# Modulation columns in 512-wide units and a new product order in the token-major groups of a hybrid decoder kernel

## The chip, the core and the metric

The kernel runs on one core of a Trainium2 chip. Time is device time of one launch in microseconds (us); the figure quoted for a kernel is the median of its runs. The core has five engines with instruction queues of their own: TensorE (PE in the rows, its weight loads as PEld), VectorE (DVE), ScalarE (ACT), GpSimd (POOL) and SyncE (SP, which here issues nearly all transfers).

## The reference, cut to what matters

One decoder layer on a sequence of 1024 tokens with 1024 features, all in 32-bit floats:

```python
mod = silu(c) @ w_ada + b_ada                    # 6 x 1024 columns of modulation
sh_a, sc_a, gt_a, sh_f, sc_f, gt_f = split(mod, 6)
h = rms_norm(x) * (1 + sc_a) + sh_a
proj = h @ w_in                                  # 9224 columns, split into:
aq, ak, av, mq, mk, mv, mo, mi, mf, ga, gm       # attention, mLSTM, gates
ya = differential_attention(aq, ak, av)
ym = sigmoid(mo) * mlstm(silu(conv(mq, mk)), mv, mi, mf)
x = x + gt_a * ((sigmoid(ga) * (ya @ w_a) + sigmoid(gm) * (ym @ w_m)) @ w_out)
h = rms_norm(x) * (1 + sc_f) + sh_f
x = x + gt_f * (relu(h @ w_ff1)**2 @ w_ff2)
```

The change touches two things: the product `h @ w_in` for the columns `mv`, `mo` and `av`, and the last 4096 of the 6144 columns of `mod` (`gt_a`, `sh_f`, `sc_f`, `gt_f`), which are needed only after the mixers.

## The kernel before

**Stages.** Up to 75.56 us the kernel normalizes x, transposes it, makes the first 2048 modulation columns (`sh_a`, `sc_a`) and, beside these, one column group of `mo` directly (`first_unit`, with its bank `ops`). From 75.56 to 306.92 five *token-major groups* (class `Tok`) compute the other columns of `mv`, `mo` and `av`. Then come eleven groups of class `Conv` and `Gate` (columns `mq`, `mk`, `ga`, `gm`, with the convolution's taps on VectorE beside them) to about 520, four mLSTM heads to about 800, eight attention heads to about 1250, the merge, and the MLP from 1430 to the end.

**A group.** Each of the groups multiplies a 1024 x 512 or 1024 x 256 block of `w_in` with h by seven half-size products in place of eight (a Strassen-type scheme, class `Group`). Products 1, 2 and 3 use quarters of the data as they are, 4 to 7 sums and differences of them, on both sides. Every operand is split into a high and a low half in TensorE's reduced 32-bit format: ScalarE copies the value into the high half (line 320), VectorE subtracts that from the value (line 138, called from `parts`). The three matmuls high x high, high x low, low x high (line 328, in `mm_block`) then give nearly full precision. In a `Tok` group a product is two halves n = 0, 1 of 24 matmuls each, 48 matmuls of 128 x 256.

**Left operands.** The weight quarters a11, a12, a21, a22 are loaded into four tiles `w_st` (line 395; two of them from a pool of two, two from the pool "b"). `weights` makes the operands in the order in which the products run: 5, 6, 3 and 7 need an addition or subtraction first (lines 411 to 419). Operands `w_op` lie in a ring of four, so operand k+4 can be made when product k has ended. The difference for product 7 goes into `cr[0]` (method `s3` of `Tok`).

**Right operands.** `B[1]` to `B[3]` are views of h transposed. Those of 7, 5, 6 and 4 are made once by `right` (lines 1393 to 1412: subtractions at line 313 on tiles `xT`, then `parts` into tiles `t7`, `t5`, `t6`, `t4`), ahead of the first group and in the same queues.

**Results.** Product 1 leaves its bank `pa` by a ScalarE copy into `m1` (line 431), and product 2 adds onto the bank. Product 7 leaves `pc` by a copy into `m7` (line 443); product 5 leaves its bank by a VectorE addition into `m7` (line 449); product 6 is added to `m1` (line 455) and yields the first output. Product 3 then accumulates on the bank `pb` of product 5, and product 4 on `pc` of product 7. The first group runs 1, 2, 7, 5, 6, 3, 4, the four others 1, 7, 2, 5, 6, 3, 4.

**Further modulation columns.** `ada_unit` (lines 695 to 740) makes 256 columns: two loads of 512 KB, each into the one buffer `cr[1]` (line 711), eight VectorE steps that multiply and add the rows into `ac` (lines 715 and 717, 256 wide), and, in `total`, a matmul with ones that sums over the partitions (line 725 or 731). There are 16 units. Fourteen are placed in the `Tok` groups, one gather for every second product; the last two stand in the first two mLSTM heads.

**What sets the order.** Every engine runs its queue in order. The order in the queues is fixed when the kernel is built: a scheduler places the instructions by program order and readiness, and pools hand out a buffer when its last reader is done. `weave` strings the steps of two lists together, here one product with one entry of `extra`.

## Time and profile before

| | |
|---|---|
| runs | 2082.44, 2076.57, 2079.22 us (median 2079.22) |
| profiled execution | 2075.06 us, its span 2073.0 us |
| mean granted clock of TensorE | 0.979 |
| TensorE busy | 1989.1 us |
| VectorE busy | 1655.4 us |
| ScalarE busy | 1045.0 us |

The span is the time from the first to the last instruction in the trace of the one execution that was profiled; that execution's own time is 2.06 us more. Times in the rows count from the start of the span. The profile gives busy time by engine and stretch, timelines of single engines, and for idle time what ended it. The granted clock is the share of TensorE's full speed that the chip's throttle allowed in a stretch.

### The profile page before, as it was taken

The numbers are of one execution on the slowest core, as the hardware profiler recorded it, in microseconds if no ns is written. First come the engines' busy times: TensorE is split into PE (matmuls) and PEld (weight loads), VectorE is DVE, ScalarE is ACT, GpSimd is POOL, SyncE is SP. The second block draws the span as 40 slices with busy tenths as digits, with TensorE's granted clock in tenths as the row PEclk, the third lists the DMA queues.
The fourth block names the chain that finished last, engine by engine and source line by source line (L and its number), as shares of the span: only waits on it lengthen the run. The fifth ranks groups of instructions, "written<-read, shape, count | busy, mean of one in ns | idle before, by whom it ended". The sixth has DMA issues, their size and how long they took to land.

```text
span 2073.0 us, 30238 instructions
## 1 busy us (share of the span) xinstructions
PE 1989.1 (96%) x11201; PEld 1723.2 (83%) x11201; DVE 1655.4 (80%) x2964; ACT 1045.0 (50%) x1966; POOL 59.3 (3%) x154
## 2 busy tenths in 40 slices
PE   5899999999999999999999899999899999999999
PEld 5899998888787899999999788777678887788887
DVE  7976768889676568999978657999867667998896
ACT  5522324544566557877767634456445445433332
POOL 0000000000011000000000110000000000000000
PEclk7999999999999999999999999999999999999999
DMA  8354452333765442322222665513444446744532
GB/s 283 107 173 157 146 180 101 102 112 134 219 207 169 138 126 54 85 77 82 62 64 85 198 226 168 185 41 112 162 153 153 146 148 235 275 154 159 163 107 77
DMA packets 210633, 296.71 MB, mean 143 GB/s; under 512 B 14067, under 2 KB 132494, under 8 KB 210486
## 3 DMA queue, kind: packets, MB, share of 16 engines
q1 hardware_dynamic: 207542, 285.35, 43.2%
q0 software_dynamic: 2944, 9.44, 1.2%
q8 instruction: 88, 1.44, 0.3%
q14 instruction: 59, 0.48, 0.1%
HBM read 206.43 MB, written 79.93 MB: 138 GB/s over the span
## 4 chain that ended last, share of the span: by engine, by line
PE 62%; DVE 15%; DMA 11%; issue 6%; ACT 4%; POOL 1%; SPq 0%; DVEq 0%; POOLq 0%; ACTq 0%
PE cps L328 15%; PE pb L328 8%; PE pc L328 7%; PE pa L328 7%; PE pd L328 4%; DMA crow<-in_w_ada_dram 4%; PE ps L166 3%; PE ps L165 3%; PE ps L167 3%; PE lg L1190 3%; PE pv L1243 3%; DVE ac L717 2%; DMA ex<-ea_d 1%; PE tp L1223 1%; PE ops L579 1%
## 5 line engine op out<-in xcount | busy, mean ns | idle before, releaser
L328 PE MATMUL cps<-t_op,s_op 128*128 128x512 f32 x2016 | 471.9, 395 | 10.6 <-ACT s_op L320 5.2
L328 PEld LDWEIGHTS cps<-t_op,s_op 128*128 128x128 f32 x2016 | 379.1, 189 | 100.8 <-ACT s_op L320 6.5
L320 ACT ACTIVATE w_op<-w_st 128x512 fp32r<-128x512 f32 (+1 forms) x192 | 130.6, 695 | 179.8 <-PE pb L328 62.6
L138 DVE TENSOR_TENSOR w_op<-w_st,w_op 128x512 fp32r<-128x512 f32 (+1 forms) x192 | 144.3, 770 | 8.3 <-ACT w_op L320 6.4
L165 PE MATMUL ps<-w_hi,hT 128*128 128x256 f32 x512 | 146.5, 286 | 0.0
L166 PE MATMUL ps<-w_lo,hT 128*128 128x256 f32 x512 | 145.9, 285 | 0.0
L167 PE MATMUL ps<-w_hi,hT 128*128 128x256 f32 x512 | 145.7, 284 | 0.0
L320 ACT ACTIVATE s_op<-act 128x1024 fp32r<-128x1024 f32 x56 | 58.6, 1052 | 143.4 <-PE cps L328 107.6
L328 PE MATMUL pc<-bt,w_op 128*128 128x512 f32 x384 | 99.8, 407 | 6.1 <-ACT w_op L320 5.1
L1200 ACT ACTIVATE ee<-ee,mneg 128x256 f32<-128x256 f32 (+7 forms) x128 | 98.2, 769 | 9.8 <-DVE mneg L1196 9.5
L1190 PE MATMUL lg<-kb,qe 128*128 128x512 f32 (+3 forms) x384 | 96.7, 360 | 3.2 <-DVE mneg L1196 2.5
L166 PEld LDWEIGHTS ps<-w_lo,hT 128*128 128x128 f32 x512 | 97.6, 191 | 1.3 <-issue 0.9
L165 PEld LDWEIGHTS ps<-w_hi,hT 128*128 128x128 f32 x512 | 97.6, 191 | 0.5
L167 PEld LDWEIGHTS ps<-w_hi,hT 128*128 128x128 f32 x512 | 97.6, 191 | 0.3
L328 PEld LDWEIGHTS pc<-bt,w_op 128*128 128x128 f32 x384 | 73.7, 195 | 27.2 <-ACT w_op L320 6.0
L328 PE MATMUL pa<-b,w_op 128*128 128x512 f32 x384 | 94.3, 396 | 0.7 <-DVE w_op L138 0.7
L316 DVE TENSOR_TENSOR acc<-cps,acc 128x512 f32<-128x512 f32 x116 | 76.9, 684 | 13.6 <-PE cps L328 13.5
L328 PEld LDWEIGHTS pa<-b,w_op 128*128 128x128 f32 x384 | 72.7, 190 | 16.1 <-DVE w_op L138 1.0
L717 DVE SCALAR_TENSOR_TENSOR ac<-crow,cond,ac 128x256 f32<-128x256 f32 x112 | 54.0, 482 | 29.5 <-DMA crow<-in_w_ada_dram 27.8
L1196 DVE CUSTOM_DVE_ANT_0 ee<-lg,bs 128x512 f32<-128x512 f32 (+4 forms) x128 | 69.9, 559 | 8.8 <-PE lg L1190 7.8
L138 DVE TENSOR_TENSOR s_op<-act,s_op 128x1024 fp32r<-128x1024 f32 x56 | 68.2, 1219 | 5.9 <-ACT s_op L320 5.9
L1190 PEld LDWEIGHTS lg<-kb,qe 128*128 128x128 f32 x384 | 61.5, 192 | 11.0 <-DVE mneg L1196 6.3
(406 smaller groups left out, 4798.8 us busy)
## 6 DMA issues: line engine op xcount, KB each, us to landing
w_st<-in_w_in_dram SPq DMA_DIRECT2D x72, 512.0 KB, 4.4
act<-act_d SPq DMA_DIRECT2D x56, 512.0 KB, 4.4
w_st<-in_w_ff_dram SPq DMA_DIRECT2D x36, 512.0 KB, 4.1
crow<-in_w_ada_dram SPq DMA_DIRECT2D x32, 512.0 KB, 4.2
w<-in_w_ff_dram SPq DMA_DIRECT2D x32, 512.0 KB, 4.9
act_d<-s SPq DMA_DIRECT2D x48, 256.0 KB, 2.0
wa<-in_w_ada_dram SPq DMA_DIRECT2D x16, 512.0 KB, 4.8
mq_d<-cv SPq DMA_DIRECT2D x16, 512.0 KB, 2.6
```

The source lines that it names most:

```text
L138: return (nc.gpsimd if pool else nc.vector).tensor_tensor(dst, src, hi.bitcast(F32), op=ALU.subtract)
L165: nc.tensor.matmul(o, lhsT=ah, rhs=bh, start=first, stop=False)
L166: nc.tensor.matmul(o, lhsT=ah, rhs=bl, start=False, stop=False)
L167: nc.tensor.matmul(o, lhsT=al, rhs=bh, start=False, stop=last)
L316: (nc.gpsimd if pick(pool, n) else nc.vector).tensor_tensor(o, a, b, op=ALU.add)
L320: nc.scalar.activation(dst[0], src, AF.Copy)
L328: nc.tensor.matmul(ps, lhsT=p, rhs=q, start=first and k == 0 and r == 0, stop=k == 3 and r == 2, skip_group_check=True,)
L717: nc.vector.scalar_tensor_tensor(ac, stv[:, k, :], cond[:, kk:kk + 1], ac, op0=ALU.mult, op1=ALU.add)
L1190: nc.tensor.matmul(lg[:, 0:max(256, w)], lhsT=hd["q"][hf][e][:, r, q4 * P:(q4 + 1) * P], rhs=hd["k"][e][:, c0:c0 + max(256, w)], start=r = ...
L1196: nc.vector.tensor_tensor_reduce(ee[:, c0:c0 + w], lg[:, 0:w], hd["bs"][:, n - c0 - w:n - c0][:, ::-1], -0.125, first, ALU.add, ALU.min, last,
L1200: nc.scalar.activation(ee[:, 0:n], ee[:, 0:n], AF.Exp, bias=mneg[:, e:e + 1], scale=-1.0, accum_out=ssum[:, e:e + 1])
L1243: nc.tensor.matmul(pv[:, 0:256], lhsT=pts[kk // 4][r][:, (kk % 4) * P:(kk % 4 + 1) * P], rhs=v, start=kk == 0 and r == 0, stop=kk == qi an ...
```

## The change

1. The further columns are made in 8 units of 512 columns. A unit has four loads of 512 KB (256 rows x 512 columns), alternately into `cr[0]` and `cr[1]`, and four `gather` steps of two VectorE instructions each, 512 wide. One load, one gather and, for every fourth, one total are placed at each product: `fetch(q)` two products ahead of `gather(q)`. Three of these steps fall into the first `Conv` group, and none is left in the mLSTM heads.
2. All `Tok` groups run the products in the order 1, 2, 5, 6, 3, 7, 4. ScalarE copies product 5 out of its bank into `m7`; VectorE adds product 7 to that from `pc`; the output that needs both is written behind product 7.
3. The difference for product 7 is made in a11's own tile (a22 - a11, where a11 holds a21 - a11 by then), so `cr[0]` is no longer used for it.
4. The first group's loads and operands are called earlier, between the calls of `right`.
5. `gate_rows` writes two tiles of 512 instead of one of 1024.

```diff
+        late7 = False
...
-                if i == 7:
+                if i == 7 and self.late7:
+                    src = a11
+                    sub(a11, a22, a11, *p, n=n)
+                elif i == 7:
...
-        gs = wt("b", [16, S], "gs")
         for i in range(2):
-            nc.scalar.copy(gs[:, i * 512:(i + 1) * 512], gps[i][0:16, :])
-        nc.sync.dma_start(gs_d, gs)
+            gs = wt("f", [16, 512], "gs")
+            nc.scalar.copy(gs, gps[i][0:16, :])
+            nc.sync.dma_start(gs_d[:, i * 512:(i + 1) * 512], gs)
...
+        def fetch(q):
+            stv = cr[q % 2].rearrange("p (k c) -> p k c", k=2)
+            src = w_ada[0][q * 256:(q + 1) * 256, c0:c0 + 512].rearrange("(k p) c -> p k c", p=P)
+            nc.sync.dma_start(stv, src)
+
+        def gather(q):
+            stv = cr[q % 2].rearrange("p (k c) -> p k c", k=2)
+            if not q:
+                box.append(wt("f", [P, 512], "ac"))
+            ac = box[0]
+            for k in range(2):
+                f = cond[:, q * 2 + k:q * 2 + k + 1]
+                if q or k:
+                    nc.vector.scalar_tensor_tensor(ac, stv[:, k, :], f, ac, op0=ALU.mult, op1=ALU.add)
+                else:
+                    nc.vector.tensor_scalar(ac, stv[:, k, :], f, None, op0=ALU.mult)
...
-        def s3(self):
-            return cr[0].rearrange("p (k c) -> p k c", k=4)
+        late7 = True
+        def p5(self):
+            for n in self.ns:
+                self.pb[n] = bank("pa", "pb5")
+                self.m7[n] = wt("m", [P, 512], "m7")
+                self.prod(5, n, self.pb[n], True)
+                nc.scalar.activation(self.m7[n], self.pb[n], AF.Copy)
+        def p6(self):
+            for n in self.ns:
+                pd, m1 = bank("mm", "pd"), self.m1[n]
+                self.prod(6, n, pd, True)
+                add(m1, pd, m1, False)
+        def p7(self):
+            for n in self.ns:
+                m7 = self.m7[n]
+                self.pc[n] = bank("pb", "pc")
+                self.prod(7, n, self.pc[n], True)
+                add(m7, self.pc[n], m7, False)
+                self.out(1, 1, n, m7, self.m1[n], m7)
...
+    ORDER_T = (1, 2, 5, 6, 3, 7, 4)
+    first_tok = Tok(*toks[0])
     right(7, "vvvv")
+    first_tok.load()
     right(5, "eeee")
+    first_tok.weights(ORDER_T[0:2])
     half(1)
     gate_rows(gps)
     right(6, "rrrr")
+    first_tok.weights(ORDER_T[2:6])
     right(4, "rruu")
+    first_tok.weights(ORDER_T[6:])
...
-    extra = [[] for _ in range(7 * len(toks))]
-    na = 0
-    while na < 16 and na * 2 + 7 < len(extra):
-        extra[na * 2].append(ada[na][0])
-        extra[na * 2 + 7].append(ada[na][1])
-        na += 1
+    extra = [[] for _ in range(7 * len(toks) + 3)]
+    for u, (fetch, gather, total) in enumerate(ada):
+        for q in range(4):
+            extra[2 + u * 4 + q].append(lambda f=fetch, q=q: f(q))
+            extra[4 + u * 4 + q].insert(0, lambda f=gather, q=q: f(q))
+        extra[8 + u * 4].insert(0, total)
...
-        more = ada[na + h::MH]
-        for u, (gather, total) in enumerate(more):
-            filler.insert(len(filler) * (2 * u + 1) // (2 * len(more) + 1), gather)
-            filler.insert(len(filler) * (2 * u + 2) // (2 * len(more) + 1), total)
```

VectorE, first group: the low half of the second product's weights (`w_op_774` before, `w_op_612` after) among the output-gate steps `mo` and the steps for right operands (`xT`, `t6`, `t4`). Before:

```order
L604 TENSOR_SCALAR mo_653<-mo_653 128x512
L604 TENSOR_SCALAR mo_689<-mo_689 128x512
L604 TENSOR_SCALAR mo_717<-mo_717 128x512
L313 TENSOR_TENSOR xT12_121<-xT12_121,xT02_119 128x1024
L313 TENSOR_TENSOR xT13_122<-xT13_122,xT03_120 128x1024
L138 TENSOR_TENSOR t6_737<-xT12_121,t6_735 128x2x256
L313 TENSOR_TENSOR xT10_123<-xT10_123,xT12_121 128x1024
L138 TENSOR_TENSOR t6_738<-xT12_121,t6_736 128x2x256
L138 TENSOR_TENSOR t6_737<-xT13_122,t6_735 128x2x256
L138 TENSOR_TENSOR t6_738<-xT13_122,t6_736 128x2x256
L313 TENSOR_TENSOR xT11_124<-xT11_124,xT13_122 128x1024
L138 TENSOR_TENSOR w_op_774<-w_st_767,w_op_774 128x1024
```

The same place after:

```order
L138 TENSOR_TENSOR w_op_612<-w_st_591,w_op_612 128x1024
L610 TENSOR_SCALAR mo_667<-mo_667 128x512
L610 TENSOR_SCALAR mo_703<-mo_703 128x512
L610 TENSOR_SCALAR mo_731<-mo_731 128x512
L313 TENSOR_TENSOR xT12_121<-xT12_121,xT02_119 128x1024
L313 TENSOR_TENSOR xT13_122<-xT13_122,xT03_120 128x1024
L138 TENSOR_TENSOR t6_753<-xT12_121,t6_751 128x2x256
L316 TENSOR_TENSOR w_st_588<-w_st_588,w_st_592 128x1024
L138 TENSOR_TENSOR t6_754<-xT12_121,t6_752 128x2x256
L138 TENSOR_TENSOR t6_753<-xT13_122,t6_751 128x2x256
L138 TENSOR_TENSOR t6_754<-xT13_122,t6_752 128x2x256
L138 TENSOR_TENSOR w_op_763<-w_st_588,w_op_763 128x1024
```

The second product's low half moved from behind eleven of these steps to ahead of them, and product 5's addition (`w_st_588`) and low half (`w_op_763`) now stand among the right operands.

VectorE, second group: reads of product 5 (`m7<-pb5`, before) and of product 7 (`m7<-pc`, after) out of their banks, between steps of the modulation columns (`ac<-crow`) and operands (`w_op`, `w_st`). Before:

```order
L717 SCALAR_TENSOR_TENSOR ac_1208<-crow_762,cond_96,ac_1208 128x256 x3
L726 TENSOR_TENSOR ac_970<-adp_1430,ac_970 128x256
L138 TENSOR_TENSOR w_op_1250<-w_st_1225,w_op_1250 128x1024
L717 SCALAR_TENSOR_TENSOR ac_1208<-crow_762,cond_96,ac_1208 128x256 x3
L316 TENSOR_TENSOR m7_1312<-pb5_1434,m7_1312 128x512
L717 SCALAR_TENSOR_TENSOR ac_1208<-crow_762,cond_96,ac_1208 128x256
L316 TENSOR_TENSOR w_st_1679<-w_st_1679,w_st_1683 128x1024
L316 TENSOR_TENSOR m7_1339<-pb5_1460,m7_1339 128x512
```

After, in the same group from product 3's second addition (`c<-pb5`) on:

```order
L316 TENSOR_TENSOR c_1503<-pb5_1367,m1_1247 128x512
L722 TENSOR_SCALAR ac_1567<-crow_796,cond_96 128x512
L138 TENSOR_TENSOR w_op_1641<-w_st_1634,w_op_1641 128x1024
L720 SCALAR_TENSOR_TENSOR ac_1567<-crow_796,cond_96,ac_1567 128x512
L313 TENSOR_TENSOR w_st_1634<-w_st_1634,w_st_1630 128x1024
L316 TENSOR_TENSOR m7_1341<-pc_1511,m7_1341 128x512
L720 SCALAR_TENSOR_TENSOR ac_1567<-crow_797,cond_96,ac_1567 128x512
L316 TENSOR_TENSOR m7_1341<-m7_1341,m1_1220 128x512
L316 TENSOR_TENSOR m7_1368<-pc_1539,m7_1368 128x512
```

VectorE no longer reads product 5 at all; it reads product 7, with single modulation steps ahead of the two reads, and those steps now come from two buffers (`crow_796`, `crow_797`).

## Rows read from the trace of the kernel before

**Rows 1.** The page's part 1: engine, busy us (share of span), instructions.

```profile
PE 1989.1 (96%) x11201; PEld 1723.2 (83%) x11201; DVE 1655.4 (80%) x2964; ACT 1045.0 (50%) x1966; POOL 59.3 (3%) x154
```

**Rows 2.** Stretches: us, busy us (instructions) by engine, granted clock, DMA share, GB/s.

```profile
95.00:310.00 215.00, 205.43 (x1643) 203.36 (x1642) 149.38 (x249) 55.52 (x74) 3.43 (x6) 0.97 0.54 167
310.00:520.00 210.00, 210.00 (x919) 172.19 (x918) 183.02 (x231) 97.58 (x137) 0.00 (x0) 1.00 0.34 114
```

**Rows 3.** The same view, two short stretches with a low granted clock.

```profile
87.92:94.85 6.93, 6.93 (x47) 6.93 (x47) 6.90 (x8) 3.09 (x4) 0.00 (x0) 0.78 0.30 89
194.80:203.83 9.03, 6.37 (x32) 6.38 (x31) 6.91 (x12) 1.75 (x3) 0.00 (x0) 0.62 0.38 117
```

**Rows 4.** TensorE's timeline, first group: start, us, instruction, count, [idle before, releaser].

```profile
75.56 6.02 PE L328 MATMUL pa<-w_op,hT 128*128 128x256 f32 x49
83.20 0.38 PE L328 MATMUL pa<-w_op,hT 128*128 128x256 f32 x1 [1.62 <-ACT m L431]
87.92 7.10 PE L328 MATMUL pa<-w_op,hT 128*128 128x256 f32 x46 [4.33 <-DVE w_op L138]
...
117.73 5.92 PE L328 MATMUL pc<-w_op,t 128*128 128x256 f32 x48
123.49 0.76 PE L328 MATMUL pa<-w_op,hT 128*128 128x256 f32 x5
```

**Rows 5.** Timelines of SyncE, ScalarE and VectorE in the first group.

```profile
74.36 0.37 SPq L395 DMA_DIRECT2D w_st<-in_w_in_dram  x1
...
78.04 1.06 ACT L320 ACTIVATE w_op<-w_st 128x1024 fp32r<-128x1024 f32 x1 [0.96 <-DMA w_st<-in_w_in_dram]
...
78.08 1.09 DVE L604 TENSOR_SCALAR mo<-mo 128x512 f32<-128x512 f32 x3
79.09 2.35 DVE L313 TENSOR_TENSOR xT<-xT,xT 128x1024 f32<-128x1024 f32 x2
...
83.10 1.89 DVE L138 TENSOR_TENSOR t<-xT,t 128x512 fp32r<-128x512 f32 x3
...
86.64 1.22 DVE L138 TENSOR_TENSOR w_op<-w_st,w_op 128x1024 fp32r<-128x1024 f32 x1
```

**Rows 6.** TensorE's timeline, the later groups.

```profile
151.74 4.73 PE L328 MATMUL pb<-w_op,hT 128*128 128x256 f32 x25 [3.94 <-DVE m L316]
...
197.48 6.51 PE L328 MATMUL pb<-w_op,hT 128*128 128x256 f32 x30 [2.66 <-DVE m L316]
...
257.25 0.58 PE L731 MATMUL adp<-ksq,ac 128*128 128x2 f32 x4 [1.37 <-DVE ac L717]
...
300.74 0.59 PE L725 MATMUL adp<-ac,ksq 128*128 128x256 f32 x2
...
306.92 2.91 PE L328 MATMUL pa<-hT,w_op 128*128 128x512 f32 x12
```

**Rows 7.** VectorE's timeline in the second group.

```profile
149.46 1.52 DVE L717 SCALAR_TENSOR_TENSOR ac<-crow,cond,ac 128x256 f32<-128x256 f32 x3 [2.99 <-DMA crow<-in_w_ada_dram]
150.91 0.68 DVE L316 TENSOR_TENSOR m<-pb,m 128x512 f32<-128x512 f32 x1
```

**Rows 8.** Waits from 75 to 310: us in total, times, longest us.

```profile
DVE ac L717 <- DMA crow<-in_w_ada_dram: 26.5, 12, 3.5
...
DVE ac L715 <- DMA crow<-in_w_ada_dram: 18.0, 9, 3.0
...
SPq L395 <- DVE ac L717: 18.1, 4, 7.3
```

**Rows 9.** Durations by line (ns min/median/max), and the page's DMA issue row.

```profile
L717 DVE SCALAR_TENSOR_TENSOR ac<-crow,cond,ac x112: 474/484/487, 99.1 to 621.6; 128x256 f32<-128x256 f32 x112
...
L789 DVE SCALAR_TENSOR_TENSOR cv<-crow,par_v,cv x48: 1274/1278/1286, 326.0 to 508.0; 128x1023 f32<-128x1023 f32 x16, 128x1022 f32<-128x1022 f32 x16, 128x1021 f32<-128x1021 f32 x16
...
crow<-in_w_ada_dram SPq DMA_DIRECT2D x32, 512.0 KB, 4.2
```

**Rows 10.** TensorE's timeline, the longest wait in the first mLSTM heads.

```profile
558.12 0.36 PE L165 MATMUL cps<-vt,kt 128*128 128x258 f32 x1 [2.54 <-DVE ex L928]
```

More of the change, by code (lines that the diff above doesn't have):

```diff
@@ new lines, in gather @@
+        def gather(q):
[9 more added lines that the diff above has]
+                    nc.vector.tensor_scalar(ac, stv[:, k, :], f, None, op0=ALU.mult)
+            if gate and q == 3:
+                br = wt("f", [P, 512], "br")
+                nc.sync.dma_start(br, bass.AP(tensor=b_ada.tensor, offset=b_ada.offset + c0, ap=[[0, P], [1, 512]]))
+                box.append(br)
@@ L721, in total @@
         def total():
[L722 removed]
+            ac = box[0]
             ps = bank("pa", "adp")
[L724 to L728 removed]
+            if gate:
+                br = box[1]
+                nc.tensor.matmul(ps, lhsT=ones, rhs=ac, start=True, stop=True)
+                nc.vector.tensor_tensor(br, ps, br, op=ALU.add)
+                i, cc = (0, u * 512) if u < 2 else (1, (u - 6) * 512)
+                nc.gpsimd.dma_start(gt_d[i, :, cc:cc + 512], br)
@@ L729, in total @@
             else:
-                for t in range(2):
+                for t in range(4):
                     nc.tensor.matmul(
@@ L1341 @@
         plan.append(lambda u=u: load_cols(w_m[0], u * 256, False))
-    ada = [ada_unit(u) for u in range(16)]
+    ada = [ada_unit(u) for u in range(8)]
     for j in range(NT + 3):
@@ L1418 @@
     right(6, "rrrr")
+    first_tok.weights(ORDER_T[2:6])
     right(4, "rruu")
+    first_tok.weights(ORDER_T[6:])
     cr = [wt("r", [P, S], "crow") for _ in range(2)]
     crow = cr
-    toks = ((("v", 0), ("v", 1)), (("v", 2), ("v", 3)), (("o", 1), ("o", 2)), (("o", 3), ("a", 0)), (("a", 1), ("a", 2)))
-    extra = [[] for _ in range(7 * len(toks))]
-    na = 0
-    while na < 16 and na * 2 + 7 < len(extra):
-        extra[na * 2].append(ada[na][0])
-        extra[na * 2 + 7].append(ada[na][1])
-        na += 1
+    extra = [[] for _ in range(7 * len(toks) + 3)]
[4 more added lines that the diff above has]
+        extra[8 + u * 4].insert(0, total)
     extra = [lambda v=v: run(v) for v in extra]
     for q, what in enumerate(toks):
+        u = Tok(*what) if q else first_tok
         if q:
-            Tok(*what).all(extra[q * 7:q * 7 + 7])
-        else:
-            Tok(*what).all(extra[0:7], (1, 2, 7, 5, 6, 3, 4))
+            u.load()
+            u.weights(ORDER_T)
+        weave([getattr(u, f"p{i}") for i in ORDER_T], extra[q * 7:q * 7 + 7])
     for v in (0, 1, "5", 2, 3, 4, "6", 5, 6, 7, "7"):
@@ L1441 @@
         del behind[:]
-        u.all([lambda n=n: run(steps[n * len(steps) // 4:(n + 1) * len(steps) // 4]) for n in range(4)] + [lambda: None] * 3)
+        steps = [lambda v=steps[n * len(steps) // 4:(n + 1) * len(steps) // 4]: run(v) for n in range(4)]
+        u.all((extra[7 * len(toks):] if v == 0 else steps) + [lambda: None] * (4 if v == 0 else 3))
     run(behind)
```

38 lines of the change are left out of this document (7 added, 31 removed).

## The prediction

> **What bounds the kernel now.** I read the page first: TensorE is busy for 1989.1 of 2073.0 us [rows 1], so an edit of VectorE work or of loads is worth only what it takes out of the 84 us in which TensorE stands still, plus what TensorE loses by a lower clock behind such a gap. Next the busy time by stretch: in the convolution groups, 310 to 520 us, TensorE has no idle time at all and VectorE fills 183 of 210 us [rows 2]; in the token-major stretch before it, 95 to 310, TensorE is idle for 9.6 us although VectorE has 149 of 215. So the change works where TensorE waits with room left on the other engines, and the question is which wait ends last there.
>
> The timeline of TensorE gives the exact account of the stage. Its first product starts at 75.56 and the first convolution product at 306.92 [rows 4, 6]: 231.4 us. An undisturbed product of 48 matmuls takes 5.76 us from start to start (117.73 to 123.49 [rows 4]), and a modulation total adds 0.42 (300.74 to 306.92 is 6.18 [rows 6]). 35 products are 201.6 us, the 14 totals of this stage about 5.6, so **24.2 us are lost**. They lie in two kinds of place.
>
> First group, 75.56 to 123.49: 47.9 us for seven products that need 40.3, so 7.6 lost. TensorE waits 1.62 us for a ScalarE copy and 4.33 for VectorE's low half of the second product's weights; the 46 matmuls behind it take 7.10 us at a granted clock of 0.78, the full speed being 1.0, where 46 at 0.12 us and a tail of 0.16 are 5.7 [rows 3, 4]. VectorE ran that low half only at 86.64 [rows 5], although its weights had been loaded from 74.36 and the high half made at 78.04: ahead of it stood the subtractions and low halves of right operands that the products 6 and 4 use much later.
>
> Groups two to five: 16.6 us lost, nearly all at three places of about 5.5 each. At 151.74 and 197.48 product 3 waits 3.94 and 2.66 us for an addition on VectorE, and the matmuls behind run slow (30 in 6.51 us, for 3.8 at full speed; granted clock 0.62 over that stretch, which is at or near the lower of the two levels for part of it) [rows 3, 6]. The third starts at 257.25 [rows 6]. VectorE's own rows say why: it stood 2.99 us until a modulation column landed, ran three of that column's steps from 149.46, and only then, at 150.91, the addition that reads product 5 out of PSUM [rows 7]; at 151.74 product 3 began to write into that bank. In the whole stretch VectorE waits 44.5 us, 21 times, for these columns [rows 8]: there is one buffer for them, a load takes 4.2 us, and it can't be issued until the four steps on the half before are done.
>
> **The change, part by part.**
>
> *First group's weights early.* By the order VectorE now has the second product's low half ahead of the three output-gate steps, that is at about 78.1 in place of 86.6. I walk on from there with the durations of before: 1.14 us for each 1024-wide step that follows another, 0.60 for a low half of a right operand, 0.34 for a gate step [rows 5]. Low half to 79.2, gate steps 80.2, two subtractions 82.5, one low half 83.1, the addition for product 5 84.3, three low halves 86.2. ScalarE, in its order, casts product 5's high half behind the copy of product 2's result for the first half, near 86.0, and takes 1.06 [rows 5]; so the low half runs from 87.1 to 88.3. TensorE ends products 1 and 2 at 75.56 + 11.5 = 87.1: it waits 1.25 us. After that the operands are ahead: product 6's low half at about 92.9 for a start at 94.1, 3's at 95.2 for 99.9, 7's at 99.4 for 105.6, 4's at 101.1 for 111.4. The group ends at 117.1 where it now ends at 123.5: **6.4 us**. Bounds: 7.6 if the wait vanishes, 0 if it grows to what it is now.
>
> *Order 1,2,5,6,3,7,4.* Product 5 is now read out by a ScalarE copy and no longer by a VectorE addition, and product 6, 5.76 us, always stands between it and product 3. The waits of 3.94 and 2.66 us have no place left. What is late next: product 4 now follows 7 directly in the same two banks, so the addition that reads half 0 of product 7 must end within half 1's 2.88 us. I walked VectorE's rows for all four changes of group: behind product 3's second addition it runs 0.34 + 1.14 + 0.75 + 1.14 us and then this addition, and is done 0.7 to 1.8 us before TensorE wants it. Product 2 now follows 1 directly too; ScalarE's copy between them is done 1.1 us ahead at the tightest, behind one weight cast.
>
> *512-wide units, two buffers.* A 256-wide step takes 484 ns and a 1023-wide one 1278 [rows 9]; on the line between them 512 is 0.75 us (bounds 0.48 and 1.28). VectorE spent 16 x 8 x 0.484 = 62 us and spends 8 x 8 x 0.75 = 48, so 14 us less, of which about 7 in this stage; it is off the path except through the waits. The loads stay 32 of 512 KB. Each is now issued about two products (11.5 us) ahead of its use and takes 4.2 [rows 9], so the 44.5 us of waiting should all but go. The third place (1.37 us and the slow matmuls behind) goes with it. On TensorE eight totals of double width replace sixteen: I take twice 0.42 each, so nothing changes in sum; seven stand in this stage, one (0.8) in the first convolution group, and the two (0.8) in the mLSTM heads go away. The last unit's steps, 2.2 us, land on VectorE in the first convolution groups, covered by its 27 us of slack there [rows 2]; uncovered they cost 2.2.
>
> *Stage sum.* 201.6 + 5.6 + 1.25, and 1.6 for four small waits at the changes of group (0.4 each, an estimate of mine with nothing like it in the rows, between bounds of 0 and 1.62, the smallest full wait in [rows 4]; 5.5 each is rival one) is 210.1. **231.4 - 210.1 = 21.3 us**.
>
> *mLSTM heads.* Two units leave: VectorE has 7.7 us less there (16 steps of 0.484 [rows 9]), and the two row buffers come free for the heads' operands. TensorE's longest wait on VectorE near them is 2.54 us [rows 10]. The order of small steps is reshuffled, so I hold 2.5 either way as the bounds and take 0.8, the two totals alone, which cancels the 0.8 of the first convolution group.
>
> *Gate rows in two halves.* One DMA more on SP, ahead of the first group's third load, and a copy moved earlier on ScalarE. That load waits in any case, to 74.36 [rows 5]. Nothing.
>
> The sum, against the profiled execution's 2075.06 us: 2053.8. The median of the three runs shown, 2079.22, lies 4.2 above that execution; from it, **2058 us**.
>
> **Rivals.**
>
> *One: VectorE's queue is late again, at another place.* The new reader of product 7 still stands behind modulation steps in an in-order queue. If a column is late there, product 4 waits as product 3 does now, at 5.5 us with the clock. In the trace 21 of the stage's 28 loads were late, by 2.1 us on average [rows 8]; against it speak the two buffers. At two of four changes of group: 10.3 us gained, 2069; at all four: 2079, nothing gained. 0.12 and 0.03. The Trainium skill, page TensorE: Matmul & The Clock Gate, section on the array of 16 blocks, says the queues of ScalarE and VectorE are strictly first in, first out, whereas TensorE's can pull weight loads ahead; it speaks against putting any step that waits for a DMA ahead of a PSUM read. The trace agrees: the addition at 150.91 ran behind a step held for 2.99 us. By that rule alone, with loads as late as now, the result would be this rival's 2079.
>
> *Two: slower.* SP issues in order, and now twelve fetches a group stand among weight loads and stores. If one of them holds a weight load until its product is late by one place in each later group, TensorE loses 5.76 us and about 1.6 of clock, four times, 29 us: 2079 - 21 + 29 = 2087. It decides when SP is held for more than about 10 us: an operand can be made three products (17.3 us) ahead, and load, cast and low half take 4.2 + 1.06 + 1.2 [rows 5, 9]. The longest hold of a weight load behind a modulation step was 7.3 us [rows 8]; fetches now wait less. 0.04.
>
> *Three: it does not do what it says* because the mLSTM heads or the convolution give the time back: a loss of 16 us or more in stretches in which TensorE is idle for little. 0.04, within 0.3%.
>
> *Four: more.* No wait left in the stage and 2.5 more in the heads: 24.2 + 2.5 - 0, so 2079.2 - 26.7 = 2052.5. 0.07.
>
> **How the numbers follow.** Forecast 0.70 (2051 to 2065: all small bounds in), rival one 0.15, two 0.04, three 0.04, four 0.07. About 0.3%, 6 us, is what a measurement of this kernel can tell from no change. Faster takes the forecast, four and rival one's first case, 0.89; same 0.07 (three, and one's second case); slower 0.04. The range, 2050 to 2070, reaches from rival four to two group ends with a wait (2069) and leaves out some 0.15.
>
> **What would show it.** Right: the first convolution product starts near 286 us; the second product of the first group starts without a gap and product 5 waits about 1 us; no wait of product 3 for an addition; VectorE's waits for the columns under 10 us; granted clock 1.0 from 95 to 285. Wrong: waits of 2 us or more of `pc` for an addition `m` (rival one), `w_op` waiting for `w_st` loads with TensorE idle (rival two), or a convolution or mLSTM stretch longer than before by over 3 us.

## The result and the profile after

The changed kernel takes **2055.39 us** (median of four runs, 2053.98 to 2057.16) against 2080.32 us in the same comparison; the ratio is 0.9891 with a 95% interval of 0.9876 to 0.9907. The prediction was 2058 us. The gain between the two medians is 24.9 us, 1.2%. The profiled execution took 2053.98 us, its span is 2052.2 us. The kernel before scatters more: over 26 runs beside the first experiments it lay between 2073.4 and 2089.4 us, and the execution whose rows stand above, 2075.06, is one of its quick ones. One execution of the experiment called e1 below, the profiled one, ran at a granted clock of 0.84 throughout and took 2195.26 us: it is left out of e1's median, and its profile serves for one wait alone.

The busy time by engine of the kernel after, against [rows 1]:

```profile
PE 1981.0 (97%) x11193; PEld 1716.0 (84%) x11193; DVE 1644.7 (80%) x2892; ACT 1046.2 (51%) x1966; POOL 56.4 (3%) x150
```

TensorE is 8 us less busy and stands still for 71 us in place of 84. By stretch the difference is plain. This is the first group, the four later groups and the convolution groups (us, busy us by engine, granted clock, DMA share, GB/s):

```profile
75.15:116.72 41.57, 40.73 (x337) 40.33 (x336) 37.97 (x49) 18.47 (x26) 0.00 (x0) 1.00 0.59 182
116.72:283.46 166.74, 166.74 (x1385) 165.30 (x1383) 120.13 (x164) 46.67 (x61) 1.80 (x3) 1.00 0.63 195
283.46:495.80 212.34, 212.34 (x928) 173.80 (x927) 187.85 (x239) 99.80 (x140) 0.54 (x1) 1.00 0.35 116
```

From the first product to the first convolution product it is 208.31 us where it was 231.36. The first group has 41.57 (47.93 before), the later four 166.74 (183.43 before), these with no idle time of TensorE at all and a granted clock of 1.00; before it was 0.97 in the nearest stretch [rows 2]. TensorE's timeline, against [rows 4, 6]:

```profile
75.15 11.90 PE L328 MATMUL pa<-w_op,hT 128*128 128x256 f32 x96
86.89 5.91 PE L328 MATMUL pb<-w_op,t 128*128 128x256 f32 x48
...
104.15 5.87 PE L328 MATMUL pc<-w_op,t 128*128 128x256 f32 x48
110.86 6.02 PE L328 MATMUL pc<-w_op,t 128*128 128x256 f32 x48 [0.84 <-DVE m L316]
116.72 11.68 PE L328 MATMUL pa<-w_op,hT 128*128 128x256 f32 x96
128.24 1.02 PE L733 MATMUL adp<-ac,ksq 128*128 128x512 f32 x2
128.70 6.23 PE L328 MATMUL pb<-w_op,t 128*128 128x256 f32 x48
...
175.78 0.95 PE L739 MATMUL adp<-ksq,ac 128*128 128x2 f32 x8
176.59 6.01 PE L328 MATMUL pd<-w_op,t 128*128 128x256 f32 x48
...
283.46 2.91 PE L328 MATMUL pa<-hT,w_op 128*128 128x512 f32 x12
```

Products 1 and 2 run as one piece, product 5 starts right behind them at 86.89, and in the whole stage there is one wait of note, 0.84 us of product 4 at 110.86. The first convolution product starts at 283.46 where it started at 306.92. VectorE's waits for columns in the stage are down from 44.5 us [rows 8] to 6.5:

```profile
DVE ac L720 <- DMA crow<-in_w_ada_dram: 6.5, 6, 2.0
```

One view of the page that the prediction does not use tells it in two lines: the chain of work that ended last (followed back from the last instruction, at each step to what released it), by engine and by line. Before:

```profile
PE 62%; DVE 15%; DMA 11%; issue 6%; ACT 4%; POOL 1%; SPq 0%; DVEq 0%; POOLq 0%; ACTq 0%
PE cps L328 15%; PE pb L328 8%; PE pc L328 7%; PE pa L328 7%; PE pd L328 4%; DMA crow<-in_w_ada_dram 4%; PE ps L166 3%; PE ps L165 3%; PE ps L167 3%; PE lg L1190 3%; PE pv L1243 3%; DVE ac L717 2%; DMA ex<-ea_d 1%; PE tp L1223 1%; PE ops L579 1%
```

After:

```profile
PE 74%; DVE 10%; DMA 7%; issue 4%; ACT 3%; POOL 1%; SPq 0%; POOLq 0%; DVEq 0%; ACTq 0%
PE cps L328 16%; PE pc L328 9%; PE pb L328 9%; PE pa L328 9%; PE pd L328 5%; PE ps L166 4%; PE ps L165 4%; PE ps L167 4%; PE lg L1219 3%; PE pv L1272 3%; DMA ex<-ea_d 2%; PE tp L1252 1%; PE ops L585 1%; DVE s_op L138 1%; DVE t_op L138 1%
```

Before, the loads of modulation columns (`DMA crow`) and their steps (`DVE ac`) are 4% and 2% of the chain, some 110 of 2073 us; over the stage alone, 75 to 310 us, the same view gives the loads 30.4%. After, the loads are not in it.

### The profile page after: what moved, and what is told of

The parts are those of the page before. It is cut to its first block, busy times and chain, and to the rows that moved or that the text cites. A ratio compares the mean times of both kernels' runs of the same rounds, so it can differ in the third digit from the quotient of the medians.

```text
span 2052.2 us, 30148 instructions
## 1 busy us (share of the span) xinstructions
PE 1981.0 (97%) x11193; PEld 1716.0 (84%) x11193; DVE 1644.7 (80%) x2892; ACT 1046.2 (51%) x1966; POOL 56.4 (3%) x150
## 4 chain that ended last, share of the span: by engine, by line
PE 74%; DVE 10%; DMA 7%; issue 4%; ACT 3%; POOL 1%; SPq 0%; POOLq 0%; DVEq 0%; ACTq 0%
PE cps L328 16%; PE pc L328 9%; PE pb L328 9%; PE pa L328 9%; PE pd L328 5%; PE ps L166 4%; PE ps L165 4%; PE ps L167 4%; PE lg L1219 3%; PE pv L1272 3%; DMA ex<-ea_d 2%; PE tp L1252 1%; PE ops L585 1%; DVE s_op L138 1%; DVE t_op L138 1%
## 5 line engine op out<-in xcount | busy, mean ns | idle before, releaser
L320 ACT ACTIVATE w_op<-w_st 128x512 fp32r<-128x512 f32 (+1 forms) x197 | 135.8, 704 | 199.4 <-PE pb L328 61.7
L138 DVE TENSOR_TENSOR w_op<-w_st,w_op 128x512 fp32r<-128x512 f32 (+1 forms) x197 | 150.4, 782 | 25.1 <-ACT w_op L320 23.1
L328 PEld LDWEIGHTS pa<-b,w_op 128*128 128x128 f32 x384 | 73.2, 192 | 15.9 <-DVE w_op L138 0.8
L328 PE MATMUL pa<-hT,w_op 128*128 128x512 f32 x264 | 64.1, 392 | 0.0
```

Of the source, the lines that this page charges most:

```text
L138: return (nc.gpsimd if pool else nc.vector).tensor_tensor(dst, src, hi.bitcast(F32), op=ALU.subtract)
L320: nc.scalar.activation(dst[0], src, AF.Copy)
L328: nc.tensor.matmul(ps, lhsT=p, rhs=q, start=first and k == 0 and r == 0, stop=k == 3 and r == 2, skip_group_check=True,)
```

## The experiments

All were compared with the kernel before, five rounds each. The table has the medians, the ratio to the kernel before with its interval, and from one profiled execution each the first group and the four later groups (first product to first product of the next).

| kernel | order | first weights | columns | median us | ratio (95%) | first group | later groups |
|---|---|---|---|---|---|---|---|
| before | old | late | 256 wide, one buffer | 2079 to 2080 | 1 | 47.93 | 183.43 |
| after | new | early | 512 wide, two buffers | 2055.39 | 0.9891 (0.9876 to 0.9907) | 41.57 | 166.74 |
| e1 | old | 1, 2 early | as before | 2079.24 | 0.9998 (0.9985 to 1.0011) | | |
| e2 | new | late | as after | 2060.41 | 0.9911 (0.9898 to 0.9924) | 49.54 | 166.74 |
| e3 | new | late | as before | 2079.39 | 1.0002 (0.999 to 1.0013) | 50.50 | 178.16 |
| e4 | old | late | 512 wide, one buffer | 2068.77 | 0.9953 (0.9934 to 0.9972) | 49.43 | 172.75 |
| e5 | new | early | 512 wide, one buffer | 2068.4 | 0.9939 (0.9917 to 0.9961) | 40.99 | 174.97 |
| e7 | new, 5 read by VectorE | early | as after | 2054.93 | 0.9883 (0.9859 to 0.9908) | 43.87 | 166.74 |
| e8 | old | late | 512 wide, two half buffers | 2061.9 | 0.9916 (0.9895 to 0.9936) | 48.93 | 166.74 |
| e9 | new | early | as before | 2081.36 | 1.0005 (0.9991 to 1.002) | 40.97 | 187.11 |
| e11 | new in group 1 only | early | as before | 2084.87 | 1.0019 (1.0003 to 1.0036) | 40.28 | 192.99 |
| e12 | old | late | as before, half the loads | 2068.7 | 0.9945 (0.9927 to 0.9963) | 48.78 | 166.66 |
| e13 | old | 1, 2 early | as before, half the loads | 2069.54 | 0.995 (0.9934 to 0.9965) | 49.44 | 166.68 |
| e14 | new in group 1 only | early | as before, half the loads | 2066.03 | 0.993 (0.9906 to 0.9954) | 40.30 | 168.43 |

The two right columns hold the answer: the later groups have a floor of 166.7 us, and whether they reach it hangs on the columns, in either order of the products (e8 and e12 against e2 and the kernel after). What the second buffer does and what the width does is not fully parted: with one buffer the wide units alone bring the later groups from 183.43 to 172.75 (e4), and 256-wide units in two buffers were not run.

**The parts alone: early weights (e1), order (e3), columns (e4), and all but the early weights (e2).** e1 takes over the calls of the first group's loads and of its first two operands:

```diff
     right(7, "vvvv")
+    first_tok.load()
     right(5, "eeee")
+    first_tok.weights((1, 2))
     half(1)
...
+            first_tok.weights((7, 5, 6, 3, 4))
```

> The kernel before, with one part of the change alone: the first group's loads are called behind the first set of right operands and the operands of products 1 and 2 behind the second (the gate rows in two halves, which free a buffer for this, come with it). Order of products, column units and everything behind are those of before. Theory of the prediction (the second product's low half stood too late in VectorE's queue, and its wait and the slow clock behind it were the whole loss of the first group): the first group takes 41.5 to 43 us in place of 47.9, the stage from the first product to the first convolution product 225 to 226.5 in place of 231.4, median 2073 to 2076. Rival (the first group gains because the new order gives product 5 more time, not because the weights are early): the group stays at 46 us or more, median 2078 to 2081.

Measured: no difference, 2079.24 us. The number falls to the rival, but for another reason than the rival's: products 1 and 2 run as one piece, and product 7 waits in place of product 2 (TensorE's timeline in e1):

```profile
93.97 0.80 PE L328 MATMUL pc<-w_op,t 128*128 128x256 f32 x2 [5.36 <-ACT w_op L320]
```

e13 below has the same wait, and its rows show what stands ahead of it.

e2 is the changed kernel with those calls undone:

```diff
     right(7, "vvvv")
-    first_tok.load()
     right(5, "eeee")
-    first_tok.weights(ORDER_T[0:2])
...
     cr = [wt("r", [P, S], "crow") for _ in range(2)]
+    first_tok.load()
+    first_tok.weights(ORDER_T)
```

> The changed kernel with one part undone: the first group's loads and all its operands are called behind the right operands, as before the change. Theory of the prediction: the first group goes back to 47 to 48 us with a wait of some 4 us ahead of the second product, the stage to 214 to 215 from 208.3, median 2060 to 2063. Rival (with the new order the early weights are worth little): group 42 to 44 us, median 2055 to 2058.

Measured: 2060.41 us, inside the range of the prediction's theory. The old wait is back, and longer than the 4 us expected: the first group takes 49.54 us, not 47 to 48, and the stage 216.28, not 214 to 215 (TensorE's timeline):

```profile
75.38 6.02 PE L328 MATMUL pa<-w_op,hT 128*128 128x256 f32 x49
...
87.95 8.49 PE L328 MATMUL pa<-w_op,hT 128*128 128x256 f32 x46 [5.60 <-DVE w_op L138]
```

So the same edit that is worth nothing in the kernel before is worth 5 us (8 in the profiles' first group) in the kernel after. That asymmetry is the thread to the cause.

e3 has the new order, with `late7`, `p5`, `p6` and `p7` of the change, on the old units:

```diff
-            Tok(*what).all(extra[0:7], (1, 2, 7, 5, 6, 3, 4))
...
+            u.weights(ORDER_T)
+        weave([getattr(u, f"p{i}") for i in ORDER_T], extra[q * 7:q * 7 + 7])
```

> The new order of products alone (with product 7's difference in a11's tile and product 5 read by ScalarE); the first group's weights late and the 256-wide column units in one buffer as before, two of them in the mLSTM heads. Theory one (the late columns at the head of VectorE's queue are the cause, and the order only moves the place): VectorE still waits about 40 us for columns, product 3's waits are gone, but product 4 waits for the addition that reads product 7 at two or more changes of group; stage 224 to 230, median 2072 to 2078. Theory two (the order alone takes the reads off the tight point, whatever the columns do): no wait over 1 us behind the first group, stage 214 to 216, median 2062 to 2065.

Measured: 2079.39 us, nothing gained; stage 228.66, in the range of theory one (the median is 1.4 us beyond it). No product 3 waits, but product 4 does, four times and 8.9 us in all. In this one profile the later groups are 5.3 us shorter than before and the first group 2.6 longer. TensorE's timeline at the worst of them, and VectorE's at the same time:

```profile
161.66 0.70 PE L731 MATMUL adp<-ac,ksq 128*128 128x256 f32 x2 [1.11 <-DVE ac L732]
162.01 0.47 PE L328 MATMUL pa<-w_op,hT 128*128 128x256 f32 x1
168.75 7.97 PE L328 MATMUL pc<-w_op,t 128*128 128x256 f32 x48 [6.27 <-DVE m L316]
```

```profile
165.76 0.35 DVE L721 TENSOR_SCALAR ac<-crow,cond 128x256 f32<-128x256 f32 x1 [1.75 <-DMA crow<-in_w_ada_dram]
166.03 0.68 DVE L316 TENSOR_TENSOR c<-pb,m 128x512 f32<-128x512 f32 x1
166.63 0.47 DVE L723 SCALAR_TENSOR_TENSOR ac<-crow,cond,ac 128x256 f32<-128x256 f32 x1
167.02 0.68 DVE L316 TENSOR_TENSOR c<-pb,m 128x512 f32<-128x512 f32 x1
167.62 0.47 DVE L723 SCALAR_TENSOR_TENSOR ac<-crow,cond,ac 128x256 f32<-128x256 f32 x1
168.01 0.68 DVE L316 TENSOR_TENSOR m<-pc,m 128x512 f32<-128x512 f32 x1
```

This is rival one of the prediction: VectorE stands 1.75 us until a column has landed, at 165.76, and only after three column steps and both additions of product 3 does it come to `m<-pc`, which product 4 has been waiting for. The landing is 1.75 of the 6.27 us; the rest is work that stands ahead in VectorE's queue.

e4 has the 512-wide units alone, through `cr[1]` only, each load one product ahead (the edit is shown against the changed kernel, whose other parts are undone as well):

```diff
-            stv = cr[q % 2].rearrange("p (k c) -> p k c", k=2)
+            stv = cr[1].rearrange("p (k c) -> p k c", k=2)
...
-            extra[2 + u * 4 + q].append(lambda f=fetch, q=q: f(q))
+            extra[3 + u * 4 + q].append(lambda f=fetch, q=q: f(q))
```

> The 512-wide units alone, in one buffer, each load called one product ahead of its steps, none left in the mLSTM heads; order of products and first group's weights as before. Theory one (late columns are the cause): VectorE's waits for columns fall from 44.5 us to under 15, product 3's waits for an addition go away with them, stage 214 to 218, median 2062 to 2067. Theory two (the order is needed, since the read of product 5 still stands behind column steps and weights in the queue): waits of product 3 of 2 us or more stay at two changes of group, stage 222 to 228, median 2070 to 2077.

Measured: 2068.77 us, later groups 172.75, stage 222.18: neither theory, for the stage is at the edge of theory two's range and the median below it. The columns are still late (VectorE waits 31.8 us for them), no product behind the first group waits for an addition, and TensorE waits at three column sums instead, 0.91, 1.54 and, in the first convolution group, 3.42 us.

**Is it a pace, not a set of places? (e11, e9, e8, e5).** With one buffer, a load can be issued only when the steps on the one before it are done. In the kernel before SyncE issued 28 of them in the stage (the row has duration in ns, first and last start):

```profile
L711 SPq DMA_DIRECT2D crow<-in_w_ada_dram x28: 367/372/570, 89.7 to 291.8; - x28
```

That is (291.8 - 89.7) / 27 = 7.5 us a load, 15.0 a unit. The stage has a unit at every second product, 2 x 5.76 + 0.42 = 11.9 us of TensorE's time. If the loads set the pace, an earlier first group gains nothing. e11 is the kernel before with the first group alone as in the change (the early calls are those of the change):

```diff
+    class TokF(Tok):
+        late7 = True      # with p5, p6 and p7 of the change
...
+    first_tok = TokF(*toks[0])
...
-            Tok(*what).all(extra[0:7], (1, 2, 7, 5, 6, 3, 4))
+            weave([getattr(first_tok, f"p{i}") for i in ORDER_T], extra[0:7])
```

> The kernel before with the first token-major group alone as in the changed kernel (weights early, order 1, 2, 5, 6, 3, 7, 4, product 7's difference in a11's tile, product 5 read by ScalarE); the other four groups and the 256-wide units in one buffer as before. Theory (early weights and the order only work together: with either of them alone one operand still stands behind all right operands): the first group takes 41 to 43 us in place of 47.9, and what follows is late by as much as before; stage 223 to 227, median 2071 to 2076. Rival (the later groups give it back, since their columns are late in any case and TensorE only reaches the same waits earlier): first group 41 to 43, but stage 228 or more, median 2077 to 2081.

Measured: 2084.87 us, 0.2% slower and 4 us beyond the rival's range; the stage, 233.26, is the rival's. By stretch, first group and later groups:

```profile
75.23:115.51 40.28, 40.28 (x337) 40.22 (x336) 39.51 (x53) 18.47 (x26) 0.00 (x0) 1.00 0.61 188
115.51:308.50 192.99, 176.97 (x1391) 174.16 (x1389) 127.99 (x219) 47.27 (x62) 3.43 (x6) 0.96 0.51 158
```

The first group takes 40.28 us with no idle time of TensorE; the later groups, in which nothing was changed, take 192.99 in place of 183.43 and so give all of it back. Its loads:

```profile
L716 SPq DMA_DIRECT2D crow<-in_w_ada_dram x28: 367/370/448, 96.1 to 293.5; - x28
```

They start later (the first one waits until 96.09 for VectorE's last low half of a right operand, which now stands behind the group's own operands), go at (293.5 - 96.1) / 27 = 7.3 us, and the last starts at 293.5, 1.7 us later than before. TensorE came 8 us earlier and waited for the same loads.

e9 adds the new order in all groups, on the old units (the changed kernel with `ada_unit`, its slots and the two units in the heads as before).

> The changed kernel with the old column units: new order and early first weights stay, but 256-wide units in one buffer, two of them in the mLSTM heads. Theory one (late columns make product 4 wait for the read of product 7, whatever the first group does): first group near 42, four to nine us of waits of product 4 for an addition and slow matmuls behind them, stage 218 to 224, median 2067 to 2075. Theory two (with the first group early the scheduler and the loads fall apart from the tight places, and the units are worth nothing): stage 209 to 213, median 2055 to 2060.

Measured: 2081.36 us. First group 40.97, later groups 187.11: both theories are missed, for the waits were not four to nine us at product 4 but some 14 us at column sums, copies and additions of several kinds. The last column load starts at 295.2. Everything but the units is there, and it is worth nothing.

e8 goes the other way: old order, late weights, and units whose rows come in 64 pieces of 256 KB into the two halves of `cr[1]`:

```diff
+        def fetch(q):
+            nc.sync.dma_start(cr[1][:, q % 2 * 512:q % 2 * 512 + 512], w_ada[0][q * P:(q + 1) * P, c0:c0 + 512])
```

> Old order of products and late first weights, with 512-wide units whose rows are loaded in 64 pieces of 256 KB into the two halves of the one row buffer, so that one piece is under way while the other is used. Theory one (what is left over in the kernel with one buffer is the late column, and two buffers heal it without the new order): VectorE's waits for columns fall under 15 us, no wait of TensorE for an addition or a column sum over 1 us behind the first group, stage 215 to 218, median 2061 to 2064. Theory two (the old order keeps some waits whatever the columns do): stage 220 or more with waits of 1 to 3 us for an addition, median 2066 to 2071.

Measured: 2061.9 us, and the later groups run at the floor:

```profile
123.25:289.99 166.74, 166.74 (x1384) 165.30 (x1383) 116.75 (x161) 47.41 (x62) 1.80 (x3) 1.00 0.61 191
```

VectorE still waits 27 us for pieces, against theory one's 15, but TensorE waits for nothing behind the first group: with two half buffers the loads keep the pace even in the old order. The stage and the median are in theory one's range. e8 and e2 differ in the order (and in how the rows are cut into loads) and have the same later groups to the hundredth.

e5 is the changed kernel with one buffer (the edit of e4).

> The changed kernel with one row buffer in place of two (each 512 KB load called one product ahead of its steps). Theory one (the second buffer is needed): VectorE waits 25 to 35 us for columns, and TensorE loses 4 to 9 us behind these at column sums or at product 4, median 2059 to 2065. Theory two (with the new order no read stands where a late column hurts, so one buffer is enough): TensorE loses less than 1.5 us more in the stage, median 2054 to 2057.

Measured: 2068.4 us, 3 beyond theory one's range; later groups 174.97, 8.2 over the floor. Its 32 loads, one for each product:

```profile
L710 SPq DMA_DIRECT2D crow<-in_w_ada_dram x32: 367/368/373, 96.3 to 296.4; - x32
```

(296.4 - 96.3) / 31 = 6.45 us a load, where a product with its share of the sums takes 166.74 / 28 = 5.96. The new order, the early weights and the wide units are all there, and the one buffer alone takes back half of the gain. The sum of a load's own parts would not tell this: 4.0 us to landing (the page's median here) and two steps of 0.75 are 5.5 us. The rest is other work of VectorE ahead of these steps.

**The pace alone (e12, e13, e14).** Three kernels leave out half of the loads (the last four steps of a unit use the first half's rows again, so the columns come out wrong) and keep everything else, the VectorE steps too:

```diff
-                nc.sync.dma_start(stv, src[:, q * 4:q * 4 + 4, :])
+                if q == 0 or u >= 14:
+                    nc.sync.dma_start(stv, src[:, q * 4:q * 4 + 4, :])
```

> The kernel before with the second load of each of the fourteen units in the token-major stage left out: the last four steps of a unit read the first half's rows again. Products, order, buffers and all VectorE steps are those of before, so only the chain of loads through the one row buffer is cut in half. Theory one (that chain, 28 times 7.5 us from 89.7 us on, sets the pace of the later groups): they take 166 to 171 us in place of 183.4, the first group about 48, median 2061 to 2066. Theory two (the later groups lose time at tight places in VectorE's queue, and the loads only add to it): 174 us or more, median 2069 to 2079.

Measured: 2068.7 us. By stretch:

```profile
74.19:122.97 48.78, 42.83 (x338) 42.42 (x337) 45.41 (x65) 18.82 (x26) 0.00 (x0) 0.93 0.52 161
122.97:289.63 166.66, 166.66 (x1391) 166.34 (x1390) 121.03 (x207) 47.49 (x62) 3.43 (x6) 1.00 0.46 138
```

The later groups stand at the floor, in the old order, with the old 256-wide steps: theory one. The median is 3 us above its range; the profile's stage is 15.9 us shorter than that of the kernel before, the medians 10.7. That the traffic is halved as well is no other explanation, since the kernel after moves all of it at the same 166.7 us.

> The same cut (no second load per unit) in the kernel with the first two products' operands early and everything else as before. Theory one (early operands for two products only move the wait to product 7, whose difference needs a row buffer that exists behind all right operands): products 1 and 2 run without a gap, product 7 waits 3 to 5 us for its operand, first group 44 to 47 us, median 2058 to 2063. Theory two (the early operands heal the first group by themselves): first group 40 to 43 us, median 2054 to 2058.

Measured: 2069.54 us, first group 49.44: theory one for the place, but nothing is gained, where 44 to 47 us and a median of 2058 to 2063 were expected. TensorE's timeline and VectorE's:

```profile
74.25 11.94 PE L328 MATMUL pa<-w_op,hT 128*128 128x256 f32 x96
91.55 0.80 PE L328 MATMUL pc<-w_op,t 128*128 128x256 f32 x2 [5.36 <-ACT w_op L320]
...
93.18 7.83 PE L328 MATMUL pc<-w_op,t 128*128 128x256 f32 x46
```

```profile
87.37 1.90 DVE L138 TENSOR_TENSOR t<-xT,t 128x512 fp32r<-128x512 f32 x3 [0.82 <-ACT t L320]
89.18 1.22 DVE L313 TENSOR_TENSOR crow<-w_st 128x1024 f32<-128x1024 f32 x1
90.44 1.22 DVE L316 TENSOR_TENSOR w_st<-w_st 128x1024 f32<-128x1024 f32 x1
91.58 1.22 DVE L138 TENSOR_TENSOR w_op<-crow,w_op 128x1024 fp32r<-128x1024 f32 x1
```

Products 1 and 2 run as one piece, and then product 7 waits 5.36 us: its difference `crow<-w_st` goes into a row buffer that is made behind all right operands, and VectorE comes to it at 89.18; ScalarE's high half of it is what ends the wait. So early weights pay only together with the order that puts product 7 sixth and its difference into a11's tile (which of these two is needed was not parted).

> The same cut (no second load per unit) in the kernel whose first group alone is as in the changed kernel; four groups in the old order, old units in one buffer. Theory one (with the chain of loads out of the way the first group's gain reaches the end, and the order of the later groups is worth nothing): first group 40 to 42 us, later groups 166 to 171, median 2053 to 2059, 6 to 8 under the kernel with the cut alone. Theory two (the first group's gain is given back in any case): 2060 to 2066.

Measured: 2066.03 us, first group 40.30, later groups 168.43. By the profile theory one holds (the stage is 6.7 us under e12's); by the medians it does not, 2.7 us under e12 with intervals that overlap, and 2066.03 is at the edge of theory two's range. The stage is settled, the rest of the kernel isn't (below).

**Who reads product 5 (e7).**

```diff
-                nc.scalar.activation(self.m7[n], self.pb[n], AF.Copy)
+                nc.vector.tensor_copy(self.m7[n], self.pb[n])
```

> The changed kernel with product 5 copied out of its bank by VectorE in place of ScalarE. Theory one (product 6 always stands between product 5 and the next use of its bank, so who reads it doesn't matter): later groups 166.7 to 168 us, median 2054 to 2058. Theory two (the read was moved to ScalarE because VectorE's queue would hold it): product 3 waits 1 us or more at two or more places, median 2058 to 2066.

Measured: 2054.93 us, theory one: the same as the change. The first group is 2.3 us longer in the one profile, which the median does not show. By stretch:

```profile
74.02:117.89 43.87, 40.71 (x337) 40.30 (x336) 38.47 (x50) 17.42 (x24) 0.00 (x0) 1.00 0.55 166
117.89:284.63 166.74, 166.74 (x1385) 165.30 (x1384) 126.17 (x173) 42.39 (x53) 1.80 (x3) 1.00 0.63 197
```

## Why the prediction was right, and where it was not

- **The sum** held: 21.3 us forecast for the stage, 23.05 measured (231.36 to 208.31); 2058 us forecast, 2055.39 measured. The way to it was half wrong, and that the sum held all the same is in part luck: the change applies the right part and the wrong ones together, so it makes no difference to the total which place is booked to which part. Some of the closeness is chance too. The profiled spans differ by 20.8 us, since the rest of the kernel took 2.2 us longer, and the medians by 24.9.
- **First group.** 6.4 forecast, 6.36 measured. The pieces differ. Product 5 does not wait 1.25 us: ScalarE's copy of the first half, behind which its cast stands, came at 84.21 and not near 86.0 (the first half of product 2 ends at three quarters of the two products), and the low half ran from 85.79, done just as TensorE came to product 5 at 86.89. Instead product 4 waits 0.84, behind an addition that stood 1.75 us until its weights landed, a wait for which the walk through VectorE's rows has no term. ScalarE's copy, and VectorE's timeline:

```profile
84.21 0.60 ACT L887 ACTIVATE c<-pa 128x512 f32<-128x512 f32 x1 [0.46 <-PE pa L328]
```

```profile
77.67 1.22 DVE L138 TENSOR_TENSOR w_op<-w_st,w_op 128x1024 fp32r<-128x1024 f32 x1
...
85.79 1.23 DVE L138 TENSOR_TENSOR w_op<-w_st,w_op 128x1024 fp32r<-128x1024 f32 x1
...
98.42 1.22 DVE L138 TENSOR_TENSOR w_op<-w_st,w_op 128x1024 fp32r<-128x1024 f32 x1
...
107.19 1.22 DVE L316 TENSOR_TENSOR w_st<-w_st 128x1024 f32<-128x1024 f32 x1 [1.75 <-DMA w_st<-in_w_in_dram]
108.33 0.74 DVE L720 SCALAR_TENSOR_TENSOR ac<-crow,cond,ac 128x512 f32<-128x512 f32 x1
108.99 1.22 DVE L138 TENSOR_TENSOR w_op<-w_st,w_op 128x1024 fp32r<-128x1024 f32 x1
110.13 0.68 DVE L316 TENSOR_TENSOR m<-pc,m 128x512 f32<-128x512 f32 x1
```

- **Order.** This step failed. "The waits of 3.94 and 2.66 us have no place left" is true, and worth nothing: with the old columns they come back at product 4 (e3), at column sums (e9), and with punctual columns the old order has no wait behind the first group either (e8, e12, e13). What the order does give is the first group: early weights in the old order gain nothing (e13: 49.44 us; with the new order in that group 40.30, e14). Rival one's condition, late columns, was the true cause in the kernel before; it got 0.15 because the units would heal it, and they did.
- **Losses as separate places.** This is the error behind it. The 7.6 us of the first group are indeed a loss of their own: with the loads halved they stay (e12, 48.78 us). But the 16.6 us of the later groups were booked at three waits, each given to the part that removes it, and they were one late chain of loads that showed at whichever place came last: take one place away (e3, e9, e11) and most or all of the time is lost at the next. The kernel's rows hinted at it. From its issue a load lands in 4.2 us and four steps take 4 x 0.48 [rows 9], 6.1 us, where TensorE uses a load in 11.9 / 2 = 5.95 us. So one buffer left no slack, and with VectorE's other work between these steps the chain went at 7.5 us before, 7.3 in e11 and 7.1 in e3.
- **The third place.** The prediction has it start at 257.25. TensorE's timeline before has five waits there, from 233.77 to 258.29 and 2.97 us in all, of which 1.37 is the one at 257.25. The 5.5 us are right as the loss of that whole stretch. It went with the columns, as forecast.
- **512-wide units.** 0.75 us for a step was forecast between 256 and 1023 columns, 747 ns is the median:

```profile
L720 DVE SCALAR_TENSOR_TENSOR ac<-crow,cond,ac x56: 741/747/754, 108.3 to 287.7; 128x512 f32<-128x512 f32 x56
```

 Waits for columns under 10 us: 6.5. On TensorE the totals were over-booked: 0.46 us for a 512-wide sum (128.24 to 128.70) and 0.81 for eight narrow ones (175.78 to 176.59), seven of them 4.6 us and not 5.6.
- **Small waits.** 1.6 us booked, 0.4 at each of four changes of group; 0.84 measured, all of it at the first of them.
- **Rival two** (weight loads held up behind fetches) does not show. The weights behind that one wait were issued at 99.67, with two column loads ahead of them in SyncE's queue (96.20 and 98.54), but what ended SyncE's wait was VectorE's low half at 98.42, shown above, which ended at 99.64. VectorE went on when they had landed, at 107.19, 7.5 us after the issue, where the median of these loads over the kernel is 4.0; why is not shown. The prediction counts twelve fetches a group; in the trace there are four to nine.

```profile
99.67 0.37 SPq L397 DMA_DIRECT2D w_st<-in_w_in_dram  x1
```

- **mLSTM heads.** 0.8 us forecast, within 2.5 either way; not settled. The pair of profiles says nothing gained (first and last start of one matmul of the heads, before and after):

```profile
L165 PE MATMUL st<-qk x64: 277/283/426, 548.9 to 749.4; 128*128 128x256 f32 x64
```

```profile
L165 PE MATMUL st<-qk x64: 274/283/418, 527.1 to 728.3; 128*128 128x256 f32 x64
```

 200.5 and 201.2 us. But over all profiles but e1's it is 200.5 to 210.0, mean 204.5, for the seven kernels that keep units in the heads, and 196.8 to 202.3, mean 199.7, for the six without: some 5 us, from one execution each. The MLP has the same instructions in all of them, and its part (last transpose ahead of it to its last product) scatters between 624.2 and 633.2 us. So what the medians of e12 to e14 lack against their stages may lie there; no run tells it apart.
- **From the profiled execution to the median** 4.2 us were added; the kernel after lies 1.4 above its own. The kernel before scattered, and its profile was a quick one.

## What to carry to other kernels

Before losses are booked place by place, look at every load-use-reload chain on a single buffer, and take its period from the trace: first and last start of the load over its count. Where that is longer than the time in which the bound engine uses one load (7.5 against 5.95 us here), expect little from a new order or a faster start alone; e3, e9 and e11 gained nothing by their medians. The sum of the parts (landing and the steps on the buffer) is only a lower bound, since other work on the engine stands between: it gave 6.1 us for 7.5 measured, and 5.5 for 6.45 in e5, where it would have said that the chain keeps up. Read the chain of work that ended last for such a transfer, over the stage in question: over the kernel it stood there with 4%, over the stage with 30.4%. And test two edits together as well as alone: here the early weights were worth 0 in one kernel and 5 us in the other.

## What the runs showed of the hardware that was not expected

The granted clock went with the waits: in the stretch of the later groups it is 1.00 in the kernel after, e2, e7, e8, e12, e13 and e14, and 0.96 in the kernel before and e11. What was not expected is that the price does not go by the length of the wait alone. Behind a wait of 4.33 us in the kernel before, 46 matmuls took 7.10 us at a granted clock of 0.78 [rows 3, 4]; behind 4.20 us in e12, in the same place, 7.94 at 0.68; behind 5.60 us in e2, 8.49 at 0.63. Behind the 0.84 us in the kernel after, the clock stayed at 1.00, and 48 matmuls took 6.02 us where 5.92 is usual.
